# A decoder layer on one core: g and b of the residual at fixed places behind weight splits, loaded in SP's queue; gate groups with a buffer for the fourth block; silu's product a unit later

## The chip, the core and the metric

The kernel runs on one core of a Trainium2 chip. Its engines work side by side and in order, each from its own list: TensorE (PE, with weight loads shown apart as PEld), VectorE (DVE), ScalarE (ACT), GpSimd (POOL) and SyncE (SP). SP here does nothing but issue transfers; POOL issues some too. The metric is the device time of one execution in microseconds (us). Before the change three runs took 1984.18, 1986.16 and 1986.17, median 1986.16.

## The reference

One decoder layer on 256 tokens of width 2048, all float32, hidden width 5632. With ALPHA a constant of about 1.19, it computes:

```
h1  = LN1(ALPHA*x  + 0.5*swiglu1(x))        swiglu(x) = (silu(x@Wgate) * (x@Wup)) @ Wdown
h2  = LN2(ALPHA*h1 + mixer(h1))
out = LN3(ALPHA*h2 + 0.5*swiglu2(h2))
mixer(h) = (sigmoid(gate_mla)*(o_mla@Wbr_mla) + sigmoid(gate_diff)*(o_diff@Wbr_diff)) @ Wout
LN(z) = (z - mean)/sqrt(var + eps) * g + b
```

`o_mla` is a multi-head latent attention with rotary positions, `o_diff` a differential attention. Their inputs and both gates are column blocks of one product, h1 @ W_in.

## The kernel before

**Weights.** The time goes into large products with weights that are read once. A weight comes in chunks of 128x1024 floats (512 KB). SP loads a chunk into one of four `raw` buffers, or into an `sraw` buffer where it is used more than once. `split` (L153) writes it as a sum of two numbers of shorter format: ACT casts the high part (L154) and DVE subtracts it for the low part (L155). The pair goes into a ring `wring` of six to ten pairs. `triple` (L206 to L209) then makes three 128x512 matmuls of each product: high by high, high by low, low by high. Activations (`x`, `xs`, `h`, `y`, `om`) are split the same way.

**Units.** The program is written as units: a load, a `prep` (the split), a `now` (the matmuls, usually 12). `look` sets how many units loads and splits run ahead. `later(n, f)` puts a piece of side work f behind the n-th unit from here. A scheduler orders each engine's list by these positions; `tc.issue_after(i)` holds an instruction behind a given one. On an engine the list is final: what waits holds up all that stands behind it.

**Groups of seven products.** For the FFNs' gate and up weights and for the mixer's gates, `Hybrid.group` (L368) replaces eight block products of 2x2 blocks by seven. The weight blocks are called 11, 12, 21 and 22; the forms 1 to 7 use them or sums of two of them, which DVE makes in place (L420). The letters of `order` (L471 to L477) are the forms, and p and q are plain units for the rest of the depth. With `small`, block 21 shares its buffers with block 12 (L360), so that it can be loaded only when 12 is done with, and form 3 stands before forms 2 and 4. The three gate groups (L1159) and three later groups of the mixer are of this kind. `sum_done` (L857 on) takes the results of a form for the FFN: DVE adds or subtracts a kept bank (`gus`), `half` lets ACT apply silu (`sg`) and DVE multiply (`hb`); `put_h` later sends the result to DRAM, turned.

**Residual.** `LayerNorm` keeps the residual rows in four tiles `z` of 128x1024. LN1's and LN2's results are stored without g and b, so the next one that takes them as its residual has to apply them: this is `pending`. `rows` loads a tile z, `gained(c)` loads g and b of column block c (`gp`, each 128x512, broadcast to all rows) and then, for each half b of the tokens, DVE computes z*g (L760) and z+b (L761) and ACT multiplies with ALPHA (L762). All of these loads are on POOL's queue (L749, L756). The places are unit counts: rows at 0, 2, 8, 10 and `gained` at 1, 6, 12, 18 for LN2; rows at 19, 21, 56, 58 and `gained` at 22, 28, 60, 68 for LN3. Later `evac` (L796, or L794 for LN2) adds the product's result to z, in order of c. In the down projection of an FFN `fold` (L779) also adds into z.

LN2's units belong to the product with Wout. Around its start the mixer ends: `branch_mla` forms, for each of four column blocks, the gated sum with DVE (`gate` L1331, `diff` L1332); PE transposes the last ones (L662), and DVE and ACT split them into `y`, the input of the same product. So at this place DVE's list mixes weight splits, the last gate products, splits of `y`, and z*g and z+b.

Of the kernel before, what the change touches and what calls it, by code (L numbers as in the profile page):

```python
# [11 lines left out]
F32 = mybir.dt.float32  # L12
# [6 lines left out]
P = 128  # L19
# [40 lines left out]
def layer_kernel(ctx: ExitStack, tc: tile.TileContext, a: dict, out: bass.AP):  # L60
# [89 lines left out]

    cast = [None]

    def split(hi, lo, src):  # L153
        cast[0] = S.copy(hi, src)  # L154
        return V.tensor_tensor(out=lo, in0=src, in1=hi.bitcast(F32), op=ALU.subtract)  # L155

# [54 lines left out]
    def project(w, x, k_tiles, width, done, k0=0, hook=None, between=None, norm=None, free=(3, 7)):  # L211
# [15 lines left out]
        def one(j):  # L227
# [3 lines left out]
            def load():  # L231
                st["raw"] = wpool.tile([P, G * width], F32, tag="raw", name=nm("raw"), bufs=4)
                for c in parts:
                    nc.sync.dma_start(st["raw"][:, c], w[j][:, c])

# [114 lines left out]
    class Hybrid:  # L350


        def __init__(self, x, seven, k_tiles, small=False, extra=None, early=()):

            line.clear()
            self.x, self.seven, self.k_tiles, self.small, self.extra = x, seven, k_tiles, small, extra
            self.early = set(early)
            self.raws = {n: early[n] if n in early else [act_tile([P, 1024], F32, "sraw") for _ in range(2)]
                         for n in ("11", "12", "22")}
            self.raws["21"] = self.raws["12"] if small else [act_tile([P, 1024], F32, "sraw") for _ in range(2)]  # L360
            if extra is not None:
                for pair in (("11", "12"), ("22", "21")):
                    t = act_tile([P, 2, 512], F32, "eraw")
                    for i, n in enumerate(pair):
                        self.raws[n] = self.raws[n] + [t[:, i, :]]
            self.snaps = [act_tile([P, 2, 512], F32, "snap") for _ in range(2)]

        def group(self, w0, w1, done, wide=False, seeded=False, gates=False):  # L368
# [72 lines left out]
            def plain(n, j, last=False):  # L441
# [4 lines left out]
                def load():  # L446
                    st["raw"] = wpool.tile([P, 1024], F32, tag="raw", name=nm("raw"), bufs=4)
                    nc.sync.dma_start(st["raw"], w[j])

# [85 lines left out]
    class Sliced:  # L535
# [8 lines left out]
        def run(self, w0, w1, units, forms, fold, done, calls, tail=0):  # L544
# [80 lines left out]
            def plain(n, j, apart):  # L625
                st = {}

                def load():
                    st["raw"] = wpool.tile([P, 1024], F32, tag="raw", name=nm("raw"), bufs=4)
                    nc.sync.dma_start(st["raw"], (w0, w1)[n][j])  # L630

# [98 lines left out]
    class LayerNorm:  # L730
        def __init__(self, scale, residual, g, bt, each, x=None, cols=None, at=((0, 2, 4, 6), (8, 11, 14, 17)), ahead=None, pending=None, due=()):
            self.scale = scale
# [14 lines left out]
            def rows(h, b):  # L747
                t = self.z[b][h] = act_tile([P, 1024], F32, "z")
                nc.gpsimd.dma_start(t, residual[b, :, h * 1024:(h + 1) * 1024])  # L749
                if pending is None:  # L750
                    later(4, lambda: S.mul(t, t, ALPHA))

            def gained(c):
                v = [tmp_tile([P, 512], "gp") for _ in range(2)]
                for t, src in zip(v, pending):
                    nc.gpsimd.dma_start(t, src[0:1, c * 512:(c + 1) * 512].partition_broadcast(P))  # L756

                def use(b):
                    z = self.z[b][c // 2][:, (c % 2) * 512:(c % 2) * 512 + 512]
                    V.tensor_tensor(out=z, in0=z, in1=v[0], op=ALU.mult)  # L760
                    V.tensor_tensor(out=z, in0=z, in1=v[1], op=ALU.add)  # L761
# [75 lines left out]
    def ffn(n, x, wgu, wdn, residual, g, bt, each, first=None, between=None, nxt=None, cols=None, norm=None, pending=None):  # L837
# [6 lines left out]

        def half(c, b, up, gate):
            q = c // 2
# [12 lines left out]
        def sum_done(c, b, bank, snap, op):  # L859
# [227 lines left out]
    def mixer(x):  # L1087
# [76 lines left out]
        def pair_cols(w, name):  # L1164
# [7 lines left out]
            return dst  # L1172

        dqT = pair_cols(a["wdq"], "dqT")
        dkT = pair_cols(a["wdk"], "dkT")
# [194 lines left out]
    def keep(i):  # L1370
        def each(b, c, z):
# [103 lines left out]
```

## Time and profile before

| | us |
|---|---|
| median of three runs | 1986.16 |
| profiled execution | 1985.03 |
| its span, first to last instruction | 1983.3 |
| PE busy / DVE busy / ACT busy / POOL busy | 1963.2 / 1759.9 / 1257.1 / 299.3 |
| mean granted clock of TensorE | 0.996 |

All times in the profile are us from the start of the span. A timeline row gives start, duration, engine, line, operation, and out<-in; in square brackets stands the idle time before it and what ended it. Rows of several like instructions are merged (xN). The durations of matmuls overlap, so their cost is the distance between starts; on DVE, too, a 128x1024 operation listed with 1.22 us starts 1.14 us before the next. SPq is SP's queue of transfers. A window row gives for each engine the busy time and the number of instructions, then the granted clock, the share of the 16 DMA engines, and GB/s.

### The profile page before, as it was taken

The page shows a single profiled execution, that of the slowest core. Times are in us where ns is not written, and L with a number is a line of the kernel's source. Part 1 is how long each engine was busy: PE and PEld are TensorE (multiplying, and loading weights), DVE is VectorE, ACT ScalarE, POOL GpSimd, SP SyncE. Part 2 cuts the span into 40 slices and gives each one's busy share as a digit, 9 for nine tenths or more (in the row PEclk, how much of TensorE's full clock was granted, in tenths as well). Part 3 has the DMA queues.
Part 4 walks back from the last instruction along what each step waited for, and adds up shares of the span by engine and source line. Part 5 has one row for each costly group of instructions (what it writes and reads, how often), then busy time and mean ns, then how long its engine had stood idle before and what let it go on. Part 6 is the DMA issues. An engine that isn't in the chain of part 4 may idle for free.

```text
span 1983.3 us, 25627 instructions
## 1 busy us (share of the span) xinstructions
PE 1963.2 (99%) x8796; PEld 1624.1 (82%) x8796; DVE 1759.9 (89%) x2143; ACT 1257.1 (63%) x1630; POOL 299.3 (15%) x523
## 2 busy tenths in 40 slices
PE   9999999999999999999999999999999999999997
PEld 8888888888888897888888887888888888888786
DVE  8899999998998879989977686689999999999986
ACT  6666666666655665666667864456676766666562
POOL 0112211122100011002223130001212121221000
PEclk9999999999999999999999999999999999999999
DMA  8878887778776666677667677578888877787763
GB/s 321 278 220 273 277 262 242 238 221 303 275 237 207 220 225 221 229 250 261 212 207 251 216 232 244 197 261 257 245 290 266 246 245 237 247 300 247 249 240 124
DMA packets 144722, 484.63 MB, mean 244 GB/s; under 512 B 20768, under 2 KB 20816, under 8 KB 144592
## 3 DMA queue, kind: packets, MB, share of 16 engines
q1 hardware_dynamic: 112752, 389.60, 56.2%
q0 software_dynamic: 31840, 93.41, 17.6%
q8 instruction: 69, 1.13, 0.2%
q14 instruction: 61, 0.50, 0.1%
HBM read 454.08 MB, written 28.84 MB: 243 GB/s over the span
## 4 chain that ended last, share of the span: by engine, by line
PE 84%; DVE 7%; issue 4%; DMA 3%; ACT 1%; POOL 1%; SPq 0%; DVEq 0%; ACTq 0%; POOLq 0%
PE mm L208 27%; PE mm L209 27%; PE mm L207 27%; DVE wring L155 3%; DMA raw<-in_dn_dram 1%; ACT wring L154 1%; DVE sraw L610 1%; PE tr L208 1%; PE tr L209 1%; PE tr L207 1%; PE tr L662 0%; DMA z<-res 0%; DMA turn<-blocks 0%; DMA sraw<-in_wgm_dram 0%; POOL turn L708 0%
## 5 line engine op out<-in xcount | busy, mean ns | idle before, releaser
L154 ACT CAST wring<-raw 128x1024 fp32r<-128x1024 f32 (+2 forms) x475 | 489.8, 1037 | 310.6 <-PE mm L209 209.2
L155 DVE TENSOR_TENSOR wring<-raw,wring 128x1024 fp32r<-128x1024 f32 (+2 forms) x475 | 566.8, 1201 | 106.6 <-ACT wring L154 104.7
L154 ACT CAST wring<-sraw 128x1024 fp32r<-128x1024 f32 x436 | 452.4, 1051 | 229.5 <-DVE sraw L420 99.9
L155 DVE TENSOR_TENSOR wring<-sraw,wring 128x1024 fp32r<-128x1024 f32 x436 | 521.6, 1219 | 30.0 <-ACT wring L154 26.7
L208 PE MATMUL mm<-wring,h 128*128 128x512 f32 (+2 forms) x1260 | 485.0, 385 | 0.2 <-DVE wring L155 0.2
L209 PE MATMUL mm<-wring,h 128*128 128x512 f32 (+2 forms) x1260 | 485.2, 385 | 0.0
L207 PE MATMUL mm<-wring,h 128*128 128x512 f32 (+2 forms) x1260 | 484.7, 385 | 0.0
L208 PE MATMUL mm<-wring,xs 128*128 128x512 f32 x776 | 302.1, 389 | 1.3 <-DVE wring L155 1.3
L207 PE MATMUL mm<-wring,xs 128*128 128x512 f32 x776 | 302.2, 389 | 0.0
L209 PE MATMUL mm<-wring,xs 128*128 128x512 f32 x776 | 301.9, 389 | 0.0
L208 PEld LDWEIGHTS mm<-wring,h 128*128 128x128 f32 x1260 | 236.7, 188 | 48.5 <-DVE wring L155 2.1
L207 PEld LDWEIGHTS mm<-wring,h 128*128 128x128 f32 x1260 | 236.7, 188 | 47.1 <-ACT h L154 0.6
L209 PEld LDWEIGHTS mm<-wring,h 128*128 128x128 f32 x1260 | 236.7, 188 | 46.8 <-DVE h L155 0.9
L420 DVE TENSOR_TENSOR sraw<-sraw,sraw 128x1024 f32<-128x1024 f32 x168 | 199.1, 1217 | 4.4 <-DMA sraw<-in_wdv_dram 2.5
L208 PEld LDWEIGHTS mm<-wring,xs 128*128 128x128 f32 x776 | 145.7, 188 | 32.1 <-DVE wring L155 1.9
L207 PEld LDWEIGHTS mm<-wring,xs 128*128 128x128 f32 x776 | 145.7, 188 | 30.1
L209 PEld LDWEIGHTS mm<-wring,xs 128*128 128x128 f32 x776 | 145.7, 188 | 30.1
L708 POOL DMA_DIRECT2D hT<-blocks x176 | 96.9, 563 | 392.4 <-DVE blocks L706 392.3
L208 PE MATMUL mm<-wring,x 128*128 128x512 f32 x348 | 135.9, 391 | 0.8 <-DVE wring L155 0.8
L207 PE MATMUL mm<-wring,x 128*128 128x512 f32 x348 | 135.5, 390 | 0.0
L209 PE MATMUL mm<-wring,x 128*128 128x512 f32 x348 | 135.3, 389 | 0.0
L422 POOL DMA_DIRECT2D sraw<-in_gu_dram x40 | 35.5, 887 | 343.0 <-DVE sraw L420 338.2
(310 smaller groups left out, 2224.5 us busy)
## 6 DMA issues: line engine op xcount, KB each, us to landing
raw<-in_gu_dram SPq DMA_DIRECT2D x167, 512.0 KB, 4.6
sraw<-in_gu_dram SPq DMA_DIRECT2D x160, 512.0 KB, 5.5
raw<-in_dn_dram SPq DMA_DIRECT2D x140, 512.0 KB, 4.8
sraw<-in_gu_dram POOLq DMA_DIRECT2D x40, 512.0 KB, 6.8
sraw<-in_dn_dram SPq DMA_DIRECT2D x36, 512.0 KB, 5.8
hraw<-hT POOLq DMA_DIRECT2D x68, 256.0 KB, 6.0
raw<-in_w_out_dram SPq DMA_DIRECT2D x32, 512.0 KB, 4.3
eraw<-in_gu_dram SPq DMA_DIRECT2D x48, 256.0 KB, 6.0
```

Source lines behind the costliest of these rows:

```text
L154: cast[0] = S.copy(hi, src)
L155: return V.tensor_tensor(out=lo, in0=src, in1=hi.bitcast(F32), op=ALU.subtract)
L207: PE.matmul(o, xh, wh, start=first, stop=False, skip_group_check=again)
L208: PE.matmul(o, xh, wl, start=False, stop=False, skip_group_check=again)
L209: PE.matmul(o, xl, wh, start=False, stop=last, skip_group_check=again)
L420: V.tensor_tensor(out=t, in0=t, in1=R[add[1]][s], op=ALU.add)
L422: nc.gpsimd.dma_start(R["12"][s], source("22", s), accum_op=ALU.add)
L610: V.tensor_tensor(out=t, in0=t, in1=held["21"] if other == "21" else R[other], op=ALU.add)
L708: nc.gpsimd.dma_start(to.rearrange("(g r) (i f) -> i r g f", g=4, i=4)[i], t[32 * i:32 * (i + 1), :].rearrange("r (g f) -> r g f", g=4))
```

## The change

**Residual.** Where `pending` is set, z and the g/b pairs are loaded by SP, each held behind the weight load issued last (`fetched`). The first z*g of each half is held behind the weight split made last (`lows`); for column block 0 of LN2 it is held behind a split of `y`, the one of quad 3 and half 1 (`past`). The second half of the tokens follows two units after the first, not one. The places move: LN2's rows to 1, 3, 11, 13 and `gained` to 2, 7, 14, 21; LN3's rows to 13, 14, 60, 62 and `gained` to 17, 32, 67, 82.

**Gates.** Block 21 has two buffers of its own until `share()`, which is called after the three gate groups. Their orders become those of the other groups, with forms 2 and 4 before 3.

**Silu.** After a `gus`, the product `hb` comes one unit later, so that a weight split stands between.

```diff
     def split(hi, lo, src):
         cast[0] = S.copy(hi, src)
-        return V.tensor_tensor(out=lo, in0=src, in1=hi.bitcast(F32), op=ALU.subtract)
+        lows[0] = V.tensor_tensor(out=lo, in0=src, in1=hi.bitcast(F32), op=ALU.subtract)
+        return lows[0]
...
-                    nc.sync.dma_start(st["raw"][:, c], w[j][:, c])
+                    fetched[0] = nc.sync.dma_start(st["raw"][:, c], w[j][:, c])
...
-            self.raws["21"] = self.raws["12"] if small else [act_tile([P, 1024], F32, "sraw") for _ in range(2)]
+            self.raws["21"] = [act_tile([P, 1024], F32, "sraw") for _ in range(2)]
+            self.shared = False
...
+        def share(self):
+            self.raws["21"] = self.raws["12"]
+            self.shared = True
...
-            if small:
+            if self.shared:
                 order = "15pp6p7p3q2q4qq" if seeded else "1p5p6p7p3q2q4qq"
             elif wide:
                 order = "15pp6p72q4q3q"
             elif seeded:
                 order = "15pp6p7p2q4q3qq"
             else:
                 order = "1p5p6p7p2q4q3qq"
...
             def rows(h, b):
                 t = self.z[b][h] = act_tile([P, 1024], F32, "z")
-                nc.gpsimd.dma_start(t, residual[b, :, h * 1024:(h + 1) * 1024])
+                src = residual[b, :, h * 1024:(h + 1) * 1024]
                 if pending is None:
+                    nc.gpsimd.dma_start(t, src)
                     later(4, lambda: S.mul(t, t, ALPHA))
+                else:
+                    with tc.issue_after(fetched[0].ins):
+                        nc.sync.dma_start(t, src)
 
             def gained(c):
                 v = [tmp_tile([P, 512], "gp") for _ in range(2)]
                 for t, src in zip(v, pending):
-                    nc.gpsimd.dma_start(t, src[0:1, c * 512:(c + 1) * 512].partition_broadcast(P))
+                    with tc.issue_after(fetched[0].ins):
+                        nc.sync.dma_start(t, src[0:1, c * 512:(c + 1) * 512].partition_broadcast(P))
 
                 def use(b):
                     z = self.z[b][c // 2][:, (c % 2) * 512:(c % 2) * 512 + 512]
-                    V.tensor_tensor(out=z, in0=z, in1=v[0], op=ALU.mult)
+                    with tc.issue_after((past() if past is not None and c == 0 else lows[0]).ins):
+                        V.tensor_tensor(out=z, in0=z, in1=v[0], op=ALU.mult)
                     V.tensor_tensor(out=z, in0=z, in1=v[1], op=ALU.add)
                     S.mul(z, z, ALPHA)
                 later(4, lambda: use(0))
-                later(5, lambda: use(1))
+                later(6, lambda: use(1))
...
-        def half(c, b, up, gate):
+        def half(c, b, up, gate, wait=0):
...
-            V.tensor_tensor(out=hb[b, q][:, o:o + 256], in0=up, in1=sg, op=ALU.mult)
+            def product():
+                V.tensor_tensor(out=hb[b, q][:, o:o + 256], in0=up, in1=sg, op=ALU.mult)
+            if wait:
+                later(wait, product)
+            else:
+                product()
...
-            half(c, b, t[:, 256:512], t[:, 0:256])
+            half(c, b, t[:, 256:512], t[:, 0:256], 1)
...
-                       ((24, 26, 48, 50) if pending is None else (19, 21, 56, 58), (94, 97, 100, 103)),
-                       35 if cols is None else None, pending, () if pending is None else (22, 28, 60, 68))
+                       ((24, 26, 48, 50) if pending is None else (13, 14, 60, 62), (94, 97, 100, 103)),
+                       35 if cols is None else None, pending, () if pending is None else (17, 32, 67, 82))
...
+        hy.share()
         dqT = pair_cols(a["wdq"], "dqT")
...
-    ln = LayerNorm(1.0, res[0], a["ln2_g"], a["ln2_b"], keep(1), h2, a["ln2_cols"], ((0, 2, 8, 10), ()), 1,
-                   (a["ln1_g"], a["ln1_b"]), (1, 6, 12, 18))
+    ln = LayerNorm(1.0, res[0], a["ln2_g"], a["ln2_b"], keep(1), h2, a["ln2_cols"], ((1, 3, 11, 13), ()), 1,
+                   (a["ln1_g"], a["ln1_b"]), (2, 7, 14, 21), lambda: yq.made[3, 1])
```

On DVE's list at the end of the mixer (`gate`, `diff`: the last gated sums; `y`: splits of their transposes; `wring`: weight splits) there stands before:

```order
L1331 TENSOR_TENSOR gate_1288_9414<-mm_1311_9520,gate_1288_9414 128x512
L155 TENSOR_TENSOR wring_3_103<-raw_1355_9699,wring_2_102 128x1024
L1332 TENSOR_TENSOR diff_1244_9126<-diff_1244_9126,gate_1288_9414 128x512
L760 TENSOR_TENSOR z_1344_9640<-z_1344_9640,gp_1346_9649 128x512
L155 TENSOR_TENSOR wring_21_121<-raw_1356_9715,wring_20_120 128x1024
L1331 TENSOR_TENSOR gate_1288_9414<-mm_1319_9557,gate_1288_9414 128x512
L761 TENSOR_TENSOR z_1344_9640<-z_1344_9640,gp_1347_9650 128x512
L1332 TENSOR_TENSOR diff_1244_9126<-diff_1244_9126,gate_1288_9414 128x512
L155 TENSOR_TENSOR y_1317_9544<-tr_1345_9642,y_1316_9543 128x512
L155 TENSOR_TENSOR wring_19_119<-raw_1357_9734,wring_18_118 128x1024
L760 TENSOR_TENSOR z_1352_9672<-z_1352_9672,gp_1346_9649 128x512
```

and now (L1350 and L1351 are the old L1331 and L1332, L772 and L773 the old L760 and L761):

```order
L1350 TENSOR_TENSOR gate_1321_9416<-mm_1344_9522,gate_1321_9416 128x512
L155 TENSOR_TENSOR wring_3_103<-raw_1388_9701,wring_2_102 128x1024
L1351 TENSOR_TENSOR diff_1277_9128<-diff_1277_9128,gate_1321_9416 128x512
L155 TENSOR_TENSOR wring_21_121<-raw_1389_9717,wring_20_120 128x1024
L1350 TENSOR_TENSOR gate_1321_9416<-mm_1352_9559,gate_1321_9416 128x512
L1351 TENSOR_TENSOR diff_1277_9128<-diff_1277_9128,gate_1321_9416 128x512
L155 TENSOR_TENSOR wring_19_119<-raw_1390_9733,wring_18_118 128x1024
L155 TENSOR_TENSOR y_1350_9546<-tr_1377_9642,y_1349_9545 128x512
L155 TENSOR_TENSOR wring_551_5064<-raw_1391_9752,wring_550_5063 128x1024
L155 TENSOR_TENSOR y_1357_9576<-tr_1385_9674,y_1356_9575 128x512
L772 TENSOR_TENSOR z_1378_9649<-z_1378_9649,gp_1381_9670 128x512
L772 TENSOR_TENSOR z_1387_9699<-z_1387_9699,gp_1381_9670 128x512
```

The z operations moved from between the last gated sums to behind the last two splits of `y`.

SP's list at the same place held weights only; now it reads as follows (`raw`: a weight chunk; the weight in the fifth row is the one that was issued at 1186.03 us before):

```order
L767 DMA gp_1381_9670<-in_ln1_g_dram 128x512
L235 DMA raw_1389_9717<-in_w_out_dram 128x1024
L235 DMA raw_1390_9733<-in_w_out_dram 128x1024
L767 DMA gp_1382_9671<-in_ln1_b_dram 128x512
L235 DMA raw_1391_9752<-in_w_out_dram 128x1024
L761 DMA z_1378_9649<-res0_100 128x1024
L761 DMA z_1387_9699<-res0_100 128x1024
L767 DMA gp_1392_9768<-in_ln1_g_dram 128x512
L767 DMA gp_1393_9769<-in_ln1_b_dram 128x512
L235 DMA raw_1396_9772<-in_w_out_dram 128x1024
L235 DMA raw_1398_9792<-in_w_out_dram 128x1024
```

Six transfers have come between the weights there.

On DVE's list in the second gate group (weights `in_wgd`; L420 before and L426 now are the sums of two blocks, `gate` the results) there stands before, up to the split at 776.73 us:

```order
L420 TENSOR_TENSOR sraw_669_5917<-sraw_669_5917,sraw_671_5919 128x1024
L155 TENSOR_TENSOR wring_520_5064<-raw_704_6148,wring_519_5063 128x1024
L1150 TENSOR_TENSOR gate_706_6194<-mm_696_6013,snap_675_5923 128x512
L155 TENSOR_TENSOR wring_19_119<-sraw_669_5917,wring_18_118 128x1024
L155 TENSOR_TENSOR wring_15_115<-raw_705_6158,wring_14_114 128x1024
L155 TENSOR_TENSOR wring_5_105<-sraw_668_5916,wring_4_104 128x1024
```

and now:

```order
L426 TENSOR_TENSOR sraw_700_5917<-sraw_700_5917,sraw_706_5923 128x1024
L155 TENSOR_TENSOR wring_3_103<-raw_736_6117,wring_2_102 128x1024
L155 TENSOR_TENSOR wring_15_115<-sraw_699_5916,wring_14_114 128x1024
L155 TENSOR_TENSOR wring_5_105<-sraw_700_5917,wring_4_104 128x1024
L1168 TENSOR_TENSOR gate_738_6162<-mm_729_6015,snap_708_5925 128x512
L155 TENSOR_TENSOR wring_21_121<-sraw_703_5920,wring_20_120 128x1024
L155 TENSOR_TENSOR wring_19_119<-sraw_704_5921,wring_18_118 128x1024
L155 TENSOR_TENSOR wring_551_5064<-raw_737_6152,wring_550_5063 128x1024
L1168 TENSOR_TENSOR gate_740_6199<-mm_730_6022,snap_707_5924 128x512
L155 TENSOR_TENSOR wring_15_115<-raw_739_6165,wring_14_114 128x1024
L155 TENSOR_TENSOR wring_5_105<-sraw_699_5916,wring_4_104 128x1024
```

The last row of each is the first split of the reloaded block 11. Form 4, which reads the block's buffers (`sraw_668`, `sraw_669` before, `sraw_699`, `sraw_700` now) before the reload, has moved ahead of form 3, whose two splits (from 703 and 704) now stand between it and the reloaded block.

More of the change, by code (lines that the diff above doesn't have):

```diff
@@ L447, in load @@
                     st["raw"] = wpool.tile([P, 1024], F32, tag="raw", name=nm("raw"), bufs=4)
-                    nc.sync.dma_start(st["raw"], w[j])
+                    fetched[0] = nc.sync.dma_start(st["raw"], w[j])
                 def prep():
@@ L629, in load @@
                     st["raw"] = wpool.tile([P, 1024], F32, tag="raw", name=nm("raw"), bufs=4)
-                    nc.sync.dma_start(st["raw"], (w0, w1)[n][j])
+                    fetched[0] = nc.sync.dma_start(st["raw"], (w0, w1)[n][j])
                 def prep():
@@ L730, in layer_kernel, with __init__ @@
     class LayerNorm:
-        def __init__(self, scale, residual, g, bt, each, x=None, cols=None, at=((0, 2, 4, 6), (8, 11, 14, 17)), ahead=None, pending=None, due=()):
+        def __init__(self, scale, residual, g, bt, each, x=None, cols=None, at=((0, 2, 4, 6), (8, 11, 14, 17)), ahead=None, pending=None, due=(), past=None):
             self.scale = scale
```

2 lines of the change are left out of this document (1 added, 1 removed).

## The prediction

> **What bounds the kernel now.** I read the page's busy times and its chain first, then the list of what TensorE waited for, then windows of 10 us around each of those waits, then the timeline of the engines there.
>
> ```profile
> PE 1963.2 (99%) x8796; PEld 1624.1 (82%) x8796; DVE 1759.9 (89%) x2143; ACT 1257.1 (63%) x1630; POOL 299.3 (15%) x523
> PE 84%; DVE 7%; issue 4%; DMA 3%; ACT 1%; POOL 1%; SPq 0%; DVEq 0%; ACTq 0%; POOLq 0%
> ...
> PE tr L662 <- DVE diff L1332: 2.8, 1, 2.8
> PE mm L208 <- DVE wring L155: 2.2, 5, 1.3
> PE tr L208 <- DVE wring L155: 1.8, 1, 1.8
> ...
> 780.00:790.00 10.00, 8.72 (x39) 6.90 (x37) 10.00 (x11) 5.73 (x7) 1.63 (x3) 1.00 0.51 173
> 1190.00:1200.00 10.00, 7.22 (x34) 5.78 (x33) 6.20 (x10) 4.34 (x6) 0.00 (x0) 0.87 1.01 375
> 1200.00:1210.00 10.00, 10.00 (x37) 8.04 (x36) 8.04 (x11) 3.69 (x6) 1.62 (x3) 0.78 0.79 258
> 1860.00:1870.00 10.00, 7.73 (x32) 5.53 (x31) 10.00 (x12) 4.94 (x5) 0.00 (x0) 1.00 0.33 112
> ```
>
> PE, the matmul engine, is busy 99% of the span, and the change takes no matmul away. It can gain only what PE loses in waits and in a lowered clock. The list of PE's waits is short (time in total, times, longest), and three of them carry nearly all of it: behind `diff`, and twice behind weight splits (`wring`). The windows (length, busy time of PE, PEld, DVE, ACT, POOL, then granted clock and DMA share) give their places: 780 to 790, 1190 to 1210, 1860 to 1870. In the second the clock falls too, to 0.87 and 0.78. In the first and last DVE is full (10.00 of 10.00); in the second it is not (6.20), and the DMA engines are (1.01).
>
> **The residual of LN2 (part A), on PE's side.** Start, duration and what ended the idle time:
>
> ```profile
> 1194.62 0.39 PE L207 MATMUL mm<-wring,y 128*128 128x512 f32 x1
> 1195.07 0.39 PE L209 MATMUL mm<-wring,y 128*128 128x512 f32 x1
> 1198.24 1.09 PE L662 MATMUL tr<-ident,diff 128*128 128x128 f32 x4 [2.78 <-DVE diff L1332]
> 1198.98 0.78 PE L207 MATMUL mm<-wring,y 128*128 128x512 f32 x1
> 1199.55 0.63 PE L208 MATMUL mm<-wring,y 128*128 128x512 f32 x1
> 1203.82 0.63 PE L209 MATMUL mm<-wring,y 128*128 128x512 f32 x1
> 1204.24 0.43 PE L207 MATMUL mm<-wring,y 128*128 128x512 f32 x1
> ```
>
> Two starts take 0.45 us between 1194.62 and 1195.07, so a matmul costs 0.227. Without the stall the four transposes would start at 1195.30. They take 0.74 at the lowered clock, so I give them half, 0.37. The twelve matmuls up to 1204.24 would take 12 x 0.227 = 2.72 in place of 5.26. That matmul would start at 1198.4, and the place loses 1204.24 - 1198.4 = 5.8 us: 2.9 before the transposes, 2.9 by the clock behind them. On DVE's side:
>
> ```profile
> 1185.67 8.70 DMA z<-res
> ...
> 1189.97 0.69 DVE L1332 TENSOR_TENSOR diff<-diff,gate 128x512 f32<-128x512 f32 x1
> 1194.46 0.69 DVE L760 TENSOR_TENSOR z<-z,gp 128x512 f32<-128x512 f32 x1 [3.80 <-DMA z<-res]
> 1195.07 1.22 DVE L155 TENSOR_TENSOR wring<-raw,wring 128x1024 fp32r<-128x1024 f32 x1
> 1196.21 0.68 DVE L1331 TENSOR_TENSOR gate<-mm,gate 128x512 f32<-128x512 f32 x1
> 1197.41 0.68 DVE L1332 TENSOR_TENSOR diff<-diff,gate 128x512 f32<-128x512 f32 x1
> ```
>
> DVE works in order. Its `z*g` stood idle 3.80 us for the residual's load, which took 8.70 us from issue, and ahead of the last `diff` product stood also a split, the gate product and `z+b`. In the new order the split, gate and `diff` follow each other with no z operation between; the first `z*g` comes behind both splits of `y`. From 1190.57 (the end of the row at 1189.97 by DVE's spacing of 0.60), one split (1.14), one gate (0.60) and `diff` (0.68) end at 1193.0, over 2 us before PE is due at 1195.30. The stall goes, and with it the fall of the clock: gain 5.8.
>
> The slow stretch follows the stall at once, and both other windows above keep clock 1.00 with shorter waits in them; so I count it to the stall. Had it another cause, only the 2.9 us of waiting would come back (a rival below). [...]
>
> What is late next? The same z loads, now in SP's queue behind a weight and `b`. In the new order they stand right behind the weight that was issued at 1186.03 (row below). Had they again 8.70 us they would land at 1194.7. The first `z*g` stands behind a split of `y` that needs PE's transposes of 1195.30, so it comes after 1196, and the margin is over 1 us. If z came later, weight splits would wait behind it on DVE, and PE would only feel it once the ring of split weights ran dry.
>
> **SP's queue, which the 24 loads enter.** It issues in order, so each load of g, b or z that waits for a buffer holds up all weights behind it.
>
> ```profile
> raw<-in_w_out_dram SPq DMA_DIRECT2D x32, 512.0 KB, 4.3
> 1186.03 0.33 SPq L234 DMA_DIRECT2D raw<-in_w_out_dram  x1
> POOL gp L756 <- DVE z L760: 11.8, 2, 11.1
> ```
>
> Weights land a median 4.3 us after issue and are issued four units ahead (four `raw` buffers). A unit is 12 matmuls, 2.72 us, so the slack is 4 x 2.72 - 4.3 = 6.6 us. On POOL one g/b load waited 11.1 us for a `z*g` to give its buffer back; such a wait on SP would be worse than the slack. In the new order the operations that free the buffers of these loads stand, on their engines, before the DVE split that releases the next weight's own buffer, so SP would be waiting anyway. So this costs 0 in the sum; at worst it is a rival. The loads' own traffic is the same bytes as before, on the same engines. Put ahead of a weight, one z (512 KB, as the weights) adds at most a weight's 4.3 us, less than 6.6. POOL loses 24 issues of about 0.5 us; it is busy 15%, worth nothing.
>
> **Gates (part B).**
>
> ```profile
> 757.60 4.63 DVE L155 TENSOR_TENSOR wring<-sraw,wring 128x1024 fp32r<-128x1024 f32 x4
> 775.64 1.05 ACT L154 CAST wring<-sraw 128x1024 fp32r<-128x1024 f32 x1 [4.08 <-DMA sraw<-in_wgd_dram]
> 776.73 1.22 DVE L155 TENSOR_TENSOR wring<-sraw,wring 128x1024 fp32r<-128x1024 f32 x1 [2.24 <-ACT wring L154]
> 788.75 1.22 DVE L155 TENSOR_TENSOR wring<-sraw,wring 128x1024 fp32r<-128x1024 f32 x1
> 788.34 0.39 PE L207 MATMUL mm<-wring,xs 128*128 128x512 f32 x1
> 790.02 0.50 PE L208 MATMUL mm<-wring,xs 128*128 128x512 f32 x1 [1.30 <-DVE wring L155]
> 790.36 0.39 PE L209 MATMUL mm<-wring,xs 128*128 128x512 f32 x1
> ```
>
> PE loses 790.36 - 788.34 - 2 x 0.227 = 1.6 us for the split of 788.75. DVE had no slack, because it had stood 2.24 us behind a cast that waited 4.08 us for the reload of block 11. That load is issued only once form 4 has read the buffer, and form 4 stood late in the order. Now form 4 comes before form 3, and block 21 has its own buffer. From the four splits at 757.60 to the awaited one the new order has 21 operations of 128x1024 (1.137 us apart) and four of 128x512 (0.60): 26.3 us, so it starts at 783.9 if nothing holds DVE, and 4.85 us earlier than 788.75 is more than the 1.6 lost. Price of the part: block 21's two loads into buffers of their own go out well ahead of this place and push plain weights behind them; two loads at a weight's 4.3 us in the row above are 8.6 at most, less than the four units, 10.9, by which plain weights run ahead. Gain 1.6; bounds 0 (another reload is late instead) and 1.6.
>
> **The last stage (parts A and C).**
>
> ```profile
> 1836.24 1.22 DVE L155 TENSOR_TENSOR wring<-raw,wring 128x1024 fp32r<-128x1024 f32 x1
> L760 DVE TENSOR_TENSOR z<-z,gp 128x512 f32<-128x512 f32 x4 | 2.7, 685 | 0.0
> L761 DVE TENSOR_TENSOR z<-z,gp 128x512 f32<-128x512 f32 x3 | 2.1, 684 | 0.0
> 1866.38 1.22 DVE L155 TENSOR_TENSOR wring<-sraw,wring 128x1024 fp32r<-128x1024 f32 x1
> 1864.49 0.39 PE L209 MATMUL mm<-wring,h 128*128 128x512 f32 x1
> 1867.65 0.50 PE L208 MATMUL tr<-wring,xs 128*128 128x512 f32 x1 [1.82 <-DVE wring L155]
> 1867.99 0.40 PE L209 MATMUL tr<-wring,xs 128*128 128x512 f32 x1
> 1910.00:1920.00 10.00, 10.00 (x46) 8.29 (x45) 7.14 (x6) 5.71 (x6) 0.53 (x1) 1.00 0.82 256
> ```
>
> PE loses 1867.99 - 1864.49 - 3 x 0.227 = 2.8 us. DVE works without a gap from 1834 and still starts the awaited split only at 1866.38. Seven of its operations (the two group rows, busy time and mean ns of one, window 1834 to 1864) are `z*g` and `z+b`: 7 x 0.60 = 4.2 us, which the change moves behind this place. One split of `h` (0.60) comes in. Counting the new order from the split at 1836.24: 17 of 1.137 and 14 of 0.60 are 27.7 us, so the awaited split starts at 1864.0, ends near 1865.2, where PE is due at about 1865.0. Gain 2.8 less some 0.3: 2.5; bounds 0 (DVE's lead was set by something earlier) and 2.8. The moved operations fall into 1880 to 1920, where DVE has idle time (2.86 us in the window quoted).
>
> The silu product one unit later puts no operation on DVE; it takes DVE's wait for ACT out of the way of a split. PE is not waiting there, so 0 either way, within the 2.2 us of all `wring` waits, of which part B already takes 1.3.
>
> **Sum.** 5.8 + 1.6 + 2.5 = 9.9 us. The profiled execution took 1985.03 us (span 1983.3), which is 1.1 below the median of the runs, 1986.16. So 1975.1 by the profiled one, 1976.3 by the median. A difference of 0.2%, 4 us, is about what a measurement of this kernel can tell from none.
>
> **Rivals.**
> 1. Only part of it comes back. If the last stage's lateness only moves (its 2.5 lost), the time is 1978.8; if the reload is late all the same, 1977.9; if the slow clock has another cause than the stall, 5.8 shrinks to 2.9 and the time is 1979.2; with the residual alone, 1980.4. For it: DVE is full at two of the places, and what leaves one place arrives in another. Against: both counts above leave time.
> 2. SP's queue stalls. It has one place, the g/b loads of the later column blocks, once in each of the two stages. If they wait there for their buffers as POOL did, 11.1 us, weights are 11.1 - 6.6 = 4.5 us late; PE stands that long and then, as at 1198, runs 2.9 us slow: 7.4 each time, 14.8 for both, less 9.9: 1991.1, slower. It decides from a wait of 6.6 us on. Against it: what frees those buffers stands ahead in the order, as said, and the pairs are five to seven units apart, 13 us and more. If it happens once, 1983.7, within 0.2%.
> 3. z lands too late for its new place on DVE, and the ring runs dry, so that the stall of 5.8 stays: 1982.1, about the bound of no change.
>
> **Chances.** Forecast (1974 to 1978.5) 0.57; rival 1 0.23; rival 2 0.13, of which 0.09 slower and 0.04 within; rival 3 0.07, half of it within 0.2%. So faster 0.83, within 0.2% 0.08, slower 0.09. The range leaves out rival 2's end and the tails: 1973.4 (a run as fast as the lowest, 1984.18, less 9.9 and less the other 0.9 of the `wring` waits, should C or a lead of DVE take them too) to 1982.
>
> **What would show it.** A: no idle PE before L662's transposes near 1195, and clock 1.00 in both windows there; the SP queue without a wait over 6.6 us at the g and b loads. B: ACT's wait of 4.08 us near 775 gone, PE busy 10.00 in 780 to 790. Last stage: no wait of PE on `wring` some 7.4 us earlier than 1865, and `z*g` rows of the second half of the columns behind it. Wrong it would be if PE's list of waits shows a new one on `wring` behind a DVE that waits for z, or behind ACT casts that wait for raw weights.

## The result, and the profile after

| | before | after |
|---|---|---|
| median of six runs, us | 1984.62 (1981.68 to 1986.17) | 1975.11 (1972.94 to 1975.91) |
| profiled execution, us | 1985.03 | 1975.91 |
| its span, us | 1983.3 | 1973.9 |

The ratio of the times is 0.9953, 95% interval 0.9940 to 0.9966: 9.5 us faster, where 9.9 were forecast, and 1975.11 lies in the forecast range. The page after, its busy times and its chain by engine:

```profile
PE 1959.4 (99%) x8796; PEld 1622.2 (82%) x8796; DVE 1759.6 (89%) x2143; ACT 1260.5 (64%) x1630; POOL 287.3 (15%) x499
PE 94%; DVE 2%; DMA 1%; ACT 1%; issue 1%; SPq 0%; POOL 0%; DVEq 0%; ACTq 0%; POOLq 0%
```

The list of what PE waited for after (time in total, times, longest):

```profile
PE tr L1265 <- DVE orow L1258: 1.4, 1, 1.4
PE tr L98 <- DVE zero L96: 1.1, 1, 1.1
PE mm L209 <- DVE wring L155: 0.8, 3, 0.4
```

PE's own share of the chain rose from 84% to 94%. The waits of before at the three places are gone from the list. Of waits for weight splits 0.8 us in all is left, and at the transposes of the attention's output rows (L1265, near 1067) stands one of 1.4 us, which had been 0.3. The windows of the three places (a place lies some us earlier now, by what was gained ahead of it):

```profile
780.00:790.00 10.00, 10.00 (x46) 8.29 (x45) 10.00 (x11) 5.50 (x6) 1.08 (x2) 1.00 0.55 202
1190.00:1200.00 10.00, 10.00 (x50) 8.29 (x49) 8.42 (x12) 4.92 (x6) 0.00 (x0) 1.00 0.94 316
1200.00:1210.00 10.00, 10.00 (x46) 8.28 (x45) 6.42 (x7) 4.56 (x7) 0.00 (x0) 1.00 0.78 256
1850.00:1860.00 10.00, 10.00 (x46) 8.29 (x45) 9.77 (x11) 6.27 (x7) 0.00 (x0) 1.00 0.59 175
```

PE is full and its clock whole in all of them. At the residual, the timeline of DVE after:

```profile
1193.39 0.69 DVE L1351 TENSOR_TENSOR diff<-diff,gate 128x512 f32<-128x512 f32 x1
1194.00 1.22 DVE L155 TENSOR_TENSOR wring<-raw,wring 128x1024 fp32r<-128x1024 f32 x1
1195.13 0.68 DVE L155 TENSOR_TENSOR y<-tr,y 128x512 fp32r<-128x512 f32 x1
1196.93 1.23 DVE L155 TENSOR_TENSOR wring<-raw,wring 128x1024 fp32r<-128x1024 f32 x1 [1.11 <-ACT wring L154]
1198.07 0.68 DVE L155 TENSOR_TENSOR y<-tr,y 128x512 fp32r<-128x512 f32 x1
1198.67 1.28 DVE L772 TENSOR_TENSOR z<-z,gp 128x512 f32<-128x512 f32 x2
```

The timeline of PE and of SP's queue there:

```profile
1186.75 0.90 SPq L761 DMA_DIRECT2D z<-res  x2
...
1195.65 0.60 PE L668 MATMUL tr<-ident,diff 128*128 128x128 f32 x4
```

The list of SP's own waits, its rows of the g and b loads over the whole program:

```profile
SPq L767 <- DMA turn<-blocks: 1.9, 1, 1.9
SPq L767 <- DVE y L155: 0.8, 1, 0.8
```

The last `diff` ends at 1194.08, 1.6 us before the transposes at 1195.65, which don't wait. The first `z*g` starts at 1198.67 without idle time: z has been there (in the trace it lands at 1192.41). SP's g and b loads waited at most 1.9 us and its z loads 0.5, far below the slack of 6.6.

To see where each microsecond went, I take the starts of all 8796 matmuls in a trace in their order and compare, over a stretch, how long the same two of them are apart in two traces. Against the profile of before, the changed kernel's PE needs:

| stretch, by the time in the trace of before | us against before |
|---|---|
| 5 to 284 (start, and the waits at 259) | +0.3 |
| 734 to 777 | +0.4 |
| 777 to 801 (gates) | -1.6 |
| 1047 to 1076 (attention's output rows) | +1.1 |
| 1184 to 1214 (residual of LN2) | -5.8 |
| 1516 to 1562 | -0.7 |
| 1845 to 1887 (last stage) | -3.1 |
| all others | +0.3 |
| sum | -9.2 |

### The profile page after: what moved, and what is told of

It reads as the page before. It is cut to its first block, busy times and chain, and to the rows that moved or that the text cites. A ratio compares the mean times of both kernels' runs of the same rounds, so it can differ in the third digit from the quotient of the medians.

```text
span 1973.9 us, 25650 instructions
## 1 busy us (share of the span) xinstructions
PE 1959.4 (99%) x8796; PEld 1622.2 (82%) x8796; DVE 1759.6 (89%) x2143; ACT 1260.5 (64%) x1630; POOL 287.3 (15%) x499
## 4 chain that ended last, share of the span: by engine, by line
PE 94%; DVE 2%; DMA 1%; ACT 1%; issue 1%; SPq 0%; POOL 0%; DVEq 0%; ACTq 0%; POOLq 0%
PE mm L209 30%; PE mm L210 30%; PE mm L208 30%; PE tr L210 1%; PE tr L209 1%; PE tr L208 1%; DVE wring L155 1%; ACT wring L154 1%; PE tr L668 0%; DMA sraw<-in_wgm_dram 0%; DVE sraw L426 0%; DMA sraw<-in_gu_dram 0%; DMA turn<-blocks 0%; PE tr L1298 0%; PE tr L1300 0%
## 5 line engine op out<-in xcount | busy, mean ns | idle before, releaser
L426 DVE TENSOR_TENSOR sraw<-sraw,sraw 128x1024 f32<-128x1024 f32 x168 | 198.4, 1214 | 3.7 <-DMA sraw<-in_wdv_dram 1.6
```

What stands on the lines that cost most here:

```text
L426: V.tensor_tensor(out=t, in0=t, in1=R[add[1]][s], op=ALU.add)
```

## The experiments

The kernels ran in three sets, beside the kernel before. Its median in these was 1984.16, 1984.40 and 1984.13, over 55 runs between 1979.66 and 1989.61. The table at the end of this section has the stretches of their traces.

### Each part alone

`gates_alone` keeps the old residual and silu:

```diff
+            self.raws["21"] = [act_tile([P, 1024], F32, "sraw") for _ in range(2)]
+            self.shared = False      # and share(), the order and its call, as in the change
```

> The kernel before with only the gate part (block 21 in buffers of its own, forms 2 and 4 before 3). Theory 1, the prediction's: the 1.6 us that PE lost at 788 come back and nothing else moves, so 1.6 us faster, PE busy 10.00 in 780 to 790. Theory 2, given back: the same 1.6 us come back at 788, but PE then reaches the transposes of the attention's output rows near 1067 earlier, and their chain on DVE hangs on transfers that PE does not speed up; PE waits there 1 to 1.5 us where it waited 0.29 before, and the net is 0.3 to 0.8 us. Theory 3: the reload is late instead, PE still idles on a weight split between 780 and 800, net 0.

1982.87 against 1984.16: 1.3 us faster, ratio 0.9987 (0.9978 to 0.9997). Its first window shows the place mended, the other two the stalls that this part doesn't touch:

```profile
780.00:790.00 10.00, 10.00 (x46) 8.27 (x45) 10.00 (x11) 6.50 (x7) 1.08 (x2) 1.00 0.55 200
1195.00:1205.00 10.00, 8.53 (x33) 7.14 (x34) 9.63 (x14) 4.59 (x6) 1.63 (x3) 0.83 0.84 308
1860.00:1870.00 10.00, 7.75 (x26) 5.68 (x25) 10.00 (x10) 5.93 (x6) 0.00 (x0) 0.83 0.46 154
```

The stretch at 788 is 1.6 us shorter, as by theory 1. Near 1067 this kernel was 0.5 us quicker than before, not slower: theory 2, that the gain is given back there, falls for this kernel.

`ln2_alone` and `ln3_alone` change one residual each:

```diff
-    ... ((0, 2, 8, 10), ()), 1, (a["ln1_g"], a["ln1_b"]), (1, 6, 12, 18))
+    ... ((1, 3, 11, 13), ()), 1, (a["ln1_g"], a["ln1_b"]), (2, 7, 14, 21), lambda: yq.made[3, 1])
```

```diff
-    (19, 21, 56, 58) ... (22, 28, 60, 68)
+    (13, 14, 60, 62) ... (17, 32, 67, 82)
```

(each with the loads on SP behind the last weight load, z*g behind the last split, and the second half two units later).

> The kernel before with only LN2's residual changed (queue, places, the hold behind the split of y). Theory 1: no wait before the diff transposes near 1195, clock 1.00 there, 5.8 us faster. Rival (the clock falls for another cause than the stall): only 2.9 us faster, with a granted clock below 1 still in 1190 to 1210. Rival (SP's queue late): a new PE wait on weight splits between 1195 and 1240, less than 3 us faster.

> The kernel before with only LN3's residual changed (queue, places). Theory 1: the seven z operations that leave DVE ahead of 1864 are what PE waited for there, so the 2.8 us wait goes to 0.3 or less: 2.5 us faster. Rival: the silu product's later place, which this kernel doesn't have, gave that place its lead; then the wait of 2.3 us idle stays above 1 us and the kernel is 0 to 1.5 us faster.

`ln2_alone`: 1980.77, 3.4 us faster, ratio 0.9981 (0.9972 to 0.9990). `ln3_alone`: 1980.96, 3.2 us faster, ratio 0.9985 (0.9975 to 0.9995). In both traces the treated place is as in the changed kernel: 5.8 us less at the residual with a whole clock, 3.1 less in the last stage. So the theory of the places holds in the trace, and for LN3 the rival, that the silu product did it, falls. But 3.4 is not 5.8. By the times alone 3.4 us (95%: 2.0 to 5.6) is nearer to the 2.9 of the rival, another cause for the slow clock, than to 5.8; what speaks against that rival is the clock, which is 1.00 at the treated place. The same two windows of `ln2_alone` show what stands against it:

```profile
1195.00:1205.00 10.00, 10.00 (x48) 8.29 (x47) 7.07 (x9) 5.62 (x7) 0.00 (x0) 1.00 0.85 307
1860.00:1870.00 10.00, 8.30 (x29) 6.68 (x30) 10.00 (x11) 6.31 (x9) 1.07 (x2) 0.83 0.69 218
```

and those of `ln3_alone`:

```profile
1195.00:1205.00 10.00, 7.91 (x30) 6.49 (x31) 9.59 (x15) 3.74 (x6) 1.63 (x3) 0.83 0.85 315
1860.00:1870.00 10.00, 10.00 (x46) 8.29 (x45) 9.68 (x11) 6.03 (x7) 2.14 (x4) 1.00 0.91 328
```

PE's first wait in `ln3_alone`:

```profile
PE tr L668 <- DVE diff L1352: 3.1, 1, 3.1
```

Where `ln2_alone` keeps the old last stage, that stage now has a clock of 0.83, which in the profile of before had been 1.00. Where `ln3_alone` keeps the old residual of LN2, its stall is longer than before (3.1 us), but the clock falls to 0.83 only, not to 0.66 as in the same window of the kernel before:

```profile
1195.00:1205.00 10.00, 7.22 (x23) 5.54 (x22) 8.97 (x13) 2.62 (x4) 1.62 (x3) 0.66 0.89 308
```

`silu_alone` moves only the product:

```diff
-            half(c, b, t[:, 256:512], t[:, 0:256])
+            half(c, b, t[:, 256:512], t[:, 0:256], 1)
```

> The kernel before with only the silu product one unit later. Theory 1, the prediction's: 0, no PE wait moves by over 0.3 us. Rival: DVE's order behind the gate and up products is better, so that the two waits on weight splits at 1541 and 1542 (0.65 us lost) go, and those at 259 to 261 (0.8 us) too: 0.6 to 1.5 us faster, and the wait at 1865 is unchanged.

1983.31, 0.85 us faster, ratio 0.9990 (0.9981 to 0.9999). The trace doesn't show from where: the waits on weight splits near 1541 are still there, that stretch is 0.65 us slower than in the profile of before, and the last stage keeps its wait. So the time lies in the rival's range without the sign that the rival named. The set below tries it again.

### What the slow clock follows

The kernels above and `sp_old_places` below give more stalls to set beside the two of before. At the residual of before the clock is 0.50 for 6.83 us:

```profile
1197.50:1204.33 6.83, 6.09 (x17) 4.96 (x18) 6.47 (x9) 2.15 (x3) 1.15 (x3) 0.50 0.85 279
```

From 1199.98 to 1203.82 the matmuls' starts lie 0.43 us apart there, against 0.227 at clock 1.00. The times at half clock in the table are worked out from the mean clock of 10 us, taking the lowered clock for 0.50 as in this row: 0.83 is (1 - 0.83) x 10 x 2 = 3.4 us, 0.66 is 6.8.

| kernel, place | PE idle, us | at half clock, us |
|---|---|---|
| before, residual of LN2 | 2.78 | 6.8 |
| gates_alone, the same | 2.7 | 3.4 |
| silu_alone, the same | 2.4 | 3.4 |
| ln3_alone, the same | 3.1 | 3.4 |
| sp_old_places, the same | 0.5 | 0 |
| before, last stage | 1.82 and 0.45 | 0 |
| gates_alone, the same | 1.8 and 0.4 | 3.4 |
| silu_alone, the same | 1.8 | 3.4 |
| ln2_alone, the same | 1.8 | 3.4 |
| sp_old_places, the same | 1.8 and 0.2 | 0 |

In the trace of before the clock is 1.00 from the start to 1197.4 and again from 1204.33 to 1970, so up to there the stretch behind the stall of 2.78 us is its only slow one. In the ten places of the table the time at half clock came to 0, 3.4 or 6.8 us. The same idle time of 1.8 us is followed by none or by 3.4, and the longest stall, 3.1 us, by 3.4, not 6.8. So the author puts the fall down to the stall, at a price that differs from trace to trace. With starts 0.43 us apart in place of 0.227, about half of the time at half clock is lost: 0, 1.7 or 3.4 us, an estimate (the trace of before shows 2.9 behind its transposes).

What sets the price is not shown. In the last stage `gates_alone` waits 1.8 and 0.4 us and has a clock of 0.83 over 10 us; `before` waits 1.82 and 0.45 us, and its clock stays 1.00. The length of the stall doesn't tell these two apart.

Two kernels were to set the length of the stall by hand:

```diff
             def done(b, bank):
                 ...
+                if (f, b) == (3, 1):
+                    for _ in range(3):        # late4: 4
+                        with tc.issue_after(last[0].ins):
+                            V.tensor_tensor(out=g0[:, b, :], in0=g0[:, b, :], in1=g0[:, b, :], op=ALU.max)
```

> The changed kernel with three needless DVE operations of 0.60 us each (gate = max(gate, gate), which changes no value) ahead of the last gate product. By the order on DVE, diff ends about 1.5 us after PE is due at 1195.6. It asks what an idle time of that length does to the clock. [...]

> As late3 with four such operations; the scheduler also puts one more weight split ahead, so diff ends about 3.2 us after PE is due. If the stall is what lowers the clock, the granted clock in 1195 to 1210 falls as it did before the change (0.87 and 0.78 in two windows of 10 us) and the place costs 3.2 us and about 3 more. If not, the clock stays 1.00 and it costs 3.2.

(`last[0]` is the `diff` product ahead of it.) They set no stall. Both took 1977.3 us in one run each, and their clock stays 1.00 from 1190 to 1205, but PE did not wait there: the scheduler put the four transposes behind more matmuls than in the changed kernel, seven in `late3` and fourteen in `late4`, where they start at 1198.11 us, after `diff` has ended at 1197.97. So they say nothing of the clock; they show that a delay on DVE that the scheduler can foresee is planned around. The stall of before hung on a transfer's landing, 8.70 us after its issue; that the scheduler did not plan for it is inferred from the stall.

### Queue or place

`pool_places` is the changed kernel with z, g and b on POOL's queue. `sp_old_places` is the kernel before with LN2's loads on SP's queue and everything else at its old place.

```diff
-                        nc.sync.dma_start(t, src)
+                        nc.gpsimd.dma_start(t, src)        # pool_places, z and g/b, both residuals
```

> The changed kernel, but z, g and b loaded by POOL's queue as before; the places and the order on DVE stay. Theory 'place': what matters is that no z operation stands ahead of the last diff product, so the gain stays whole, 9 to 10 us faster than before, within 1.5 us of the changed kernel. Theory 'queue': on POOL the loads wait for buffers (11.1 us before) and land late again, DVE waits for z behind the splits of y and the ring runs dry; at least 3 us slower than the changed kernel, with PE idle on a weight split between 1198 and 1215.

> The kernel before, only with LN2's z, g and b loaded by SP's queue behind the last weight load; unit counts and the order on DVE as before, z*g ahead of the last gate and diff products. Theory 'place': the stall stays, since diff still stands behind a wait for z: 0 to 2 us faster. Theory 'queue': in the changed kernel z landed 5.7 us after its issue at 1186.75, at 1192.4, not 8.7; with that, z*g would run at 1192.4 and diff end near 1195, in time for PE's 1195.3: the stall of 2.78 falls below 0.5 and the kernel is 5 us faster.

`pool_places`: 1974.45 against 1984.40, ratio 0.9954 (0.9939 to 0.9969), the same as the changed kernel's. A row of its waits near the residual:

```profile
POOL gp L769 <- DVE z L774: 23.1, 2, 12.8
```

and its windows there:

```profile
1190.00:1200.00 10.00, 10.00 (x50) 8.29 (x49) 8.45 (x12) 4.75 (x6) 0.54 (x1) 1.00 1.02 397
1200.00:1210.00 10.00, 10.00 (x46) 8.29 (x45) 6.22 (x7) 5.28 (x6) 0.54 (x1) 1.00 0.84 293
```

POOL's queue waits for buffers for up to 12.8 us, longer than before (11.1), and PE doesn't feel it: from 1183 to 1200 POOL's list holds only these loads, and PE needs 5.8 us less than before from 1184 to 1214, as in the changed kernel. So theory 'place' holds, and the move to SP's queue was not needed for the gain.

`sp_old_places` went 1982.40 against 1984.40, ratio 0.9989 (0.9978 to 1.0000), runs from 1979.7 to 1984.7. The timeline of its DVE at the place:

```profile
1192.80 0.69 DVE L774 TENSOR_TENSOR z<-z,gp 128x512 f32<-128x512 f32 x1 [1.44 <-DMA gp<-in_ln_b_dram]
1193.41 0.68 DVE L1351 TENSOR_TENSOR gate<-mm,gate 128x512 f32<-128x512 f32 x1
1194.01 0.68 DVE L775 TENSOR_TENSOR z<-z,gp 128x512 f32<-128x512 f32 x1
1194.61 0.68 DVE L1352 TENSOR_TENSOR diff<-diff,gate 128x512 f32<-128x512 f32 x1
```

and PE's wait there:

```profile
PE tr L668 <- DVE diff L1352: 0.5, 1, 0.5
```

The first row names a load of `gp`; z's own load, which the operation needs too, was there by then. In this execution `z*g` started at 1192.80, sooner than before (1194.46), and the stall was 0.5 us, near what theory 'queue' said. It took 1979.71 us, though, the shortest of the ten runs; by the median 2.0 us were gained, not 5, which theory 'place' allowed. So neither theory is borne out whole: with the earlier landing the stall was shorter in this execution (0.5 us for 2.78), but `diff` still stands behind it, and only the new place took it away. How long the stall was in the other nine runs isn't known, since one execution is profiled.

### The parts taken out of the change

```diff
+            self.raws["21"] = self.raws["12"] if small else [...]     # no_gates: the old groups
-            half(c, b, t[:, 256:512], t[:, 0:256], 1)                   # no_silu
+            half(c, b, t[:, 256:512], t[:, 0:256])
```

`residuals_only` has both; `changed_again` has neither.

> The changed kernel with the silu product back at its old place. Theory 'silu is worth nothing': within 0.7 us of the changed kernel that runs beside it, and in the trace no PE wait near 1541 or 1865 beyond what the changed kernel shows. Rival (silu alone had come out 0.85 us faster by its median): 0.7 to 1.5 us slower than the changed kernel, with a wait on weight splits back at 1541 and 259.

> The changed kernel with the old gate groups. Theory 1: 1.0 to 1.6 us slower than the changed kernel, all of it at 788, where the unchanged gate groups of the other runs lost 0.9 to 1.6. Rival (given back at 1067): PE's wait at the transposes near 1067 falls from 1.43 us idle to 0.3 or less and the kernel is only 0 to 0.5 us slower.

> The changed kernel's program unchanged, beside the three others of this set, as their measure: 9 to 10 us faster than before. If PE's wait of 1.43 us near 1067 belongs to the changed order it is there again; if it is a matter of when a transfer lands, it differs by up to 1 us.

> The kernel before with both residuals changed, LN2's and LN3's, and neither the gates nor silu. If the parts add up: slower than the changed kernel by the gates' 1.0 to 1.6 us and silu's 0, so 8 to 9 us faster than before. By the sum of the two medians alone (3.4 and 3.2 us) it would be 6.6 us faster; more than that would say that the stalls of before in those runs were shorter than typical, or that one stall hides the other's cost.

| kernel | median, us | runs, us | ratio to before (95%) |
|---|---|---|---|
| before | 1984.13 | 1980.64 to 1987.59 | |
| changed_again | 1973.76 | 1973.50 to 1974.47 | 0.9949 (0.9937 to 0.9961) |
| no_silu | 1974.27 | 1972.52 to 1979.25 | 0.9954 (0.9941 to 0.9967) |
| no_gates | 1976.38 | 1975.66 to 1976.64 | 0.9961 (0.9949 to 0.9973) |
| residuals_only | 1975.97 | 1974.49 to 1978.65 | 0.9957 (0.9944 to 0.9970) |

`changed_again` was 10.4 us faster than before, a little more than expected, and its wait near 1067 was 0.8 us, not 1.43, so that wait varies between executions of one program. Silu's shift is worth 0.5 us by the medians, with runs that overlap on both sides: not told from nothing. The gates are worth 2.6 us by the medians, more than either theory expected; by the stretches 1.6 at 788, about 1 in the first 284 us, and smaller pieces that go both ways. The wait near 1067 did fall to 0.2 us without them, as the rival said, and yet the kernel was slower by more than its 0 to 0.5 us. Both residuals together bring 8.2 us, as expected, and more than the 6.6 of the two alone; the intervals of these numbers, 1.8 to 2.6 us to either side, leave room for that. That the clock differs between executions may be another reason; no run shows it.

The stretches, us against the profile of before. The columns leave out 284 to 777, 1076 to 1184, 1214 to 1516 and what follows 1887; the first moves by some 0.2 with the matmul at which it starts. A stretch that a kernel left as it was still differs by up to 1.6 us between executions, and twice by 4 us (see the end):

```
                 5-284  777-801  801-1047  1047-1076  1184-1214  1516-1562  1562-1845  1845-1887    all
changed           +0.3     -1.6      +0.1       +1.1       -5.8       -0.7       +0.0       -3.1   -9.2
changed_again     -0.3     -1.6      +0.2       +0.5       -5.8       -0.6       +0.0       -3.1  -10.6
pool_places       +0.1     -1.6      +0.0       -0.2       -5.8       -0.0       +0.0       -3.1  -10.3
no_silu           -0.3     -1.6      +3.9       -0.1       -5.8       +0.6       +0.4       -3.1   -5.7
no_gates          +0.8     +0.0      +0.1       -0.2       -5.8       +0.0       +0.0       -3.1   -8.5
residuals_only    +0.2     -0.3      +4.0       -0.4       -5.8       -0.9       -0.0       -3.1   -6.5
gates_alone       +0.2     -1.6      +0.6       -0.5       -1.5       -0.8       +1.0       +1.3   -1.6
silu_alone        -0.3     -0.4      +0.0       -0.5       -1.6       +0.7       +1.3       +0.7   -0.3
ln2_alone         +0.4     -0.2      +0.0       +0.1       -5.8       -0.4       +0.9       +0.9   -4.3
ln3_alone         -0.9     -0.6      +0.3       -0.5       -0.9       +0.5       +0.0       -3.1   -5.0
sp_old_places     +0.2     +0.0      +0.1       -0.5       -5.1       -0.8       +1.4       -0.5   -5.5
```

## Why the prediction was right, point by point

**The residual of LN2, 5.8.** Right in its mechanism and, against the trace it was read from, to the tenth: the stall and the fall of the clock that followed it are gone. `diff` no longer stands behind a load, z was issued at 1186.75 behind the weight as reckoned, and `z*g` came 4 us after the estimated landing at 1194.7. The half of it that was clock, 2.9, is not a constant, though. In the three other traces that keep the old residual the place lost 4.2 to 4.9 us (5.8 less 1.6 and less 0.9), with 3.4 us at half clock each, not 6.8, and run against run the part alone brought 3.4 (2.0 to 5.6). So 5.8 was read from an execution that lost more there than the three others. The rival that the slow clock has another cause is out: with no stall the clock there is 1.00 (`ln2_alone`, `pool_places` and the changed kernel, in the windows above), and the stretch takes the same 5.8 us less in seven traces of seven with LN2's new places and no stall added (`ln2_alone`, `pool_places`, the changed kernel twice, `no_silu`, `no_gates`, `residuals_only`).

**SP's queue, 0.** Right, and the rival of a stalled queue is out: 1.9 us was its longest wait at a g or b load. That the loads go to this queue at all was not needed (`pool_places`); the prediction had not said which half of the part would bring the time.

**The gates, 1.6.** Right at the place, 1.6 in every kernel that has them. The awaited split was reckoned for 783.9; it started near 785.7, because DVE still waited once, 1.19 us, behind a cast of a reloaded block, and the whole place came 0.6 later. The timeline after, of ACT and DVE:

```profile
776.58 1.05 ACT L154 CAST wring<-sraw 128x1024 fp32r<-128x1024 f32 x1 [2.57 <-DMA sraw<-in_wgd_dram]
777.67 1.23 DVE L155 TENSOR_TENSOR wring<-sraw,wring 128x1024 fp32r<-128x1024 f32 x1 [1.19 <-ACT wring L154]
785.69 1.21 DVE L155 TENSOR_TENSOR wring<-sraw,wring 128x1024 fp32r<-128x1024 f32 x1
```

So "the reload is late" was half true, within the margin. Block 11 and its forms lost no PE time by it.

**The last stage, 2.5.** Right in its mechanism, too small in size. The 0.3 us that were to remain did not: the place gives all its 2.8 us and 0.3 of small ones before it, because DVE, with less to do, ran ahead until it waited for its ring (idle 1.49 us for ACT at 1837.88), a lead that a count from the old starting time could not have. The timeline of DVE after:

```profile
1837.88 1.23 DVE L155 TENSOR_TENSOR wring<-raw,wring 128x1024 fp32r<-128x1024 f32 x1 [1.49 <-ACT wring L154]
```

From there to 1866 no `z*g` or `z+b` stands on DVE's timeline any more. The larger miss was to take the loss of before from one execution. The four other traces with the old last stage lost 0.9 to 2.3 us more in 1562 to 1887 than that one: a wait of 0.6 to 0.7 us near 1790 that it did not have, and in three of them the clock (0.83 over 10 us). Against those four the last stage was worth 4.0 to 5.4, against the profile of before 3.1, not 2.5.

**Silu, 0.** `silu_alone` came out 0.85 us faster, but the undoing, `no_silu`, gives 0.5 with overlapping runs. The stretch from 1516 to 1562, where a rival looked for its worth, does not follow it: -0.7 to +0.65 us with the shift, -0.9 to +0.6 without. A few tenths can't be told.

**The sum.** 9.9 forecast, 9.5 to 10.4 measured in the two sets with the changed program. Two terms were off in opposite ways: the residual cost less than 5.8 in other executions, the last stage more than 2.5. That the total came out so near owes something to luck. The medians of the parts alone, 3.4, 1.3, 3.2 and 0.85, add up to 8.8.

**What the prediction did not have.** PE's wait of 1.4 us near 1067. There a DVE transpose (L712) needs one of six small buffers, which is free only when the transfers out of it have landed. In the changed kernel's trace the last of them was issued at 1048.34, 0.8 us earlier than before, and landed at 1054.08, 0.3 later, so the output rows came no sooner while PE came 0.9 us sooner. Four traces with the whole change and the loads on SP (two of them `late3` and `late4`, at +0.5 each) have 0.5 to 1.1 us more there than before, and all others -0.5 to +0.1 (`no_silu` came there 4 us late for another reason, below). The gates alone don't cause it, and whether the loads on SP do is not settled.

## What to carry to other kernels

Where an engine that works in order feeds the bound, look at what stands ahead of the awaited instruction and waits for something else: here moving that one operation behind took away a wait of 2.78 us and, with the clock, 5.8 us at the place, on SP's queue and on POOL's. The stall of 2.78 us cost 2.9 us more by the clock in the profile of before, while a wait of 1.8 us was followed by no slow clock in two traces and by 3.4 us of it in three; so price a stall from several profiles, not one. The changed kernel may also be steadier: its eleven runs (loads on SP) lay within 3 us, the 55 of before in the three sets within 10. But more runs spread wider, and `no_silu`, without the stalls of LN2 and the last stage, still spread over 6.7 us.

## What the runs showed of the hardware

After the same idle time of 1.8 us in the last stage the clock stayed 1.00 in two traces and was lowered in three, to 0.83 over 10 us, which is 3.4 us at half speed. In `no_silu` and `residuals_only` PE lost 4 us in a stretch that no kernel here sets out to change and that cost at most 0.6 in the others: it waited 2.0 and 2.1 us for columns of `dk` that come back from a turn through DRAM, and in `residuals_only` the clock was 0.85 over the 10 us of the wait. PE's wait in `residuals_only`, and ACT's wait, in the stretch from 925 to 955, for a transfer of the `dq` columns ahead of it:

```profile
PE tr L1226 <- ACT dkT L734: 2.1, 1, 2.1
...
ACT dqT L734 <- DMA turned<-turn: 3.9, 1, 3.9
```

Its window there, with the clock at 0.85:

```profile
945.00:955.00 10.00, 7.89 (x30) 6.10 (x29) 10.00 (x13) 4.70 (x6) 4.63 (x9) 0.85 0.48 125
```

The profiled executions of these two kernels, 1979.25 and 1978.65, were the slowest of their runs, with medians of 1974.27 and 1975.97; so most of their runs will not have had it, which is inferred from the times. That the late transfer of `dq` is what made `dk` late is argued: between the two stand ACT's casts of weights, which came late after it. Why a transfer of 256 KB landed late in just these executions stays open.
